# Longer contiguous runs for the expert weight loads of a hybrid encoder block with a mixture of experts

## Chip, cores and metric

One core of one Trainium2 chip runs the whole block, one layer, batch 1, 1,024 tokens of width 1,024, in float32. The metric is the device time of one execution in microseconds, as the median over runs.

## What is computed

The first half of the block mixes tokens (an input projection, a convolution branch, a gated linear attention branch, an output projection, a layer norm). The second half is a hierarchical mixture of experts: each token picks one group of 8 experts and in it 2 of 8 experts. Each of the 64 experts is a SwiGLU network with w1 and w3 of 1024 x 512 and w2 of 512 x 1024. The change touches this half alone.

```python
def hier_moe(x, w_rg, b_rg, w_re, b_re, w1, w3, w2):
    ...
    def expert_block(args):
        xb, e = args
        hdn = jax.nn.silu(xb @ w1[e]) * (xb @ w3[e])
        return hdn @ w2[e]
    ys = lax.map(expert_block, (xs, block_e)).reshape(n_slots, d) * slot_w[:, None]
    out = jnp.zeros((n_tok, d), x.dtype).at[slot_tok].add(ys)
```

## The kernel before

The engines run in program order; semaphores tie them together. The mixing half and the router take about the first 1,035 us. From then on the kernel goes through 29 tiles of 128 token rows in a fixed order (PATTERN). A tile holds one expert with 128 rows (letters r and o), two with 64 rows (s and d) or four with 32 rows (q). The 64 experts are ranked by their token counts on the chip, and the rank decides which of the three capacities an expert gets; 32 experts have 32 rows. One expert with more than 128 rows continues in the first d tile.

**Weights.** An expert's weights are six pieces of 1 MB: two of w1, two of w3, two of w2, in this order (w_pieces, line 924). load_piece (line 931) sends one piece into one of 22 slots of 128 partitions x 8 KB, some 16 of which serve the weights at a time. A half of w1 or w3 is 512 rows of 512 numbers: partition p gets rows p, 128 + p, 256 + p and 384 + p, each a run of 2 KB in memory. A half of w2 is 256 rows of 1,024 numbers: partition p gets rows p and 128 + p, each a run of 4 KB. pump_w (line 971) issues the next pieces on SyncE's queue as soon as TensorE has released as many slots: one after each quarter of a job's w1 and w3 products, two after its w2 products.

**A tile's tokens.** prep (line 1363) clears xgp and gathers the tile's 128 token rows into it from memory with an indirect DMA of GpSimd, one tile ahead. make_xt (line 1200) turns xgp into xT with eight 128 x 128 transposes on TensorE: transpose k takes columns k*128 to k*128 + 127, so that xT[:, k] has the inputs which the k-th 128 rows of w1 and w3 need. In a transpose the data is the loaded (stationary) operand.

**A job** is one expert on its rows. With T = 128 / rows (1, 2 or 4), job_h (line 1375) computes for each of 8 steps k and each of T column tiles j the product of xT[:, k] (stationary) with n = 512 / T columns of w1, then of w3; the column tile j writes its own 128 / T partitions of PSUM, so that the hidden columns j*n to (j+1)*n stand in the j-th partition group (line 1420). Each float32 product is two passes in the trace. ScalarE and VectorE then form silu(h1) * h3 in hs. job_t (line 1430) transposes hs in 4 / T pieces of 128 columns, and job_y (line 1438) multiplies with w2: step f takes the f-th 128 hidden numbers and the f-th 128 rows of w2. Transposes, w2 products and the scatter of finished tiles of the job before (combine, line 1487: products of one-hot matrices that add into the residual rows) are issued in between the 16 steps of the next job_h.

The last tile is a q tile. Its rows are finished apart (begin_last, add_last, last_rows), while the layer norm of all other rows goes out.

Of the kernel before, what the change touches and what calls it, by code (L numbers as in the profile page):

```python
# [28 lines left out]
DE = 512  # L29
# [25 lines left out]
assert (1 + N64) % 2 == 0 and N32 % 4 == 0  # L55
OVB = NT * 128
RND = float(3 << 22)


def _order():  # L60
# [22 lines left out]
def tile_block(ctx: ExitStack, tc: tile.TileContext, x, w_in, b_in, conv_w, conv_b, conv_ln_g,  # L83
# [5 lines left out]
    out = out[0]  # L89
# [13 lines left out]
    def slot(dt, name):  # L103
        return SP.tile([128, 2048], dt, tag="slot", name=name, bufs=NS)
# [13 lines left out]
    TE = nc.tensor  # L118
# [13 lines left out]
    ident = CP.tile([128, 128], F32, name="ident")  # L132
# [117 lines left out]
    def load_x(i):  # L250
        t = slot(F32, f"x{i}")
        for c in (slice(0, 512), slice(512, DM)) if i < 2 else (slice(0, DM),):
# [9 lines left out]
                      in_=w_in[:, C_F:C_F + 16].rearrange("(k p) c -> p k c", p=128))  # L262
# [606 lines left out]
    def mmb(shape=(128, 512), name="psb"):  # L869
        return PB.tile(list(shape), F32, tag="mm", name=name, bufs=5)  # L870
# [60 lines left out]
    def load_piece(wt, pc, t=None, eng=nc.sync):  # L931
        nm, src, i, e = pc
        if t is None:
            t = slot(F32, f"{nm}_{i}")
        if isinstance(e, int):
            m = src[e:e + 1]
        else:
            m = src[bass.ds(e(), 1)]
        r = 512 if nm != "w2" else 256
        f = 512 if nm != "w2" else 1024  # L940
        eng.dma_start(out=t.rearrange("p (k f) -> p k f", f=f),  # L941
                          in_=m.rearrange("o r f -> (o r) f")[i * r:(i + 1) * r].rearrange("(k p) f -> p k f", p=128))
        wt.setdefault(nm, []).append(t)

    rank_reg = {}
# [25 lines left out]
    def pump_w(eng=nc.sync):  # L971
        while queue and free[0] > 0 and (queue[0][0][0] == "s" or known):
            key, pc = queue.popleft()
            load_piece(wts_of[key], pc, eng=eng)
            free[0] -= 1
# [128 lines left out]
    xgp = CB.tile([128, DM], F32, name="xgp")  # L1104
# [95 lines left out]
    def make_xt(xT):  # L1200
        for h in range(2):
            ps = mmb((128, 4, 128), "psxT")
            for k in range(4):
                TE.transpose(ps[:, k, :], xgp[:, (4 * h + k) * 128:(4 * h + k + 1) * 128], ident)  # L1204
            A.copy(xT[:, 4 * h:4 * h + 4, :], ps)  # L1205

    static_map(0)
# [42 lines left out]
    V.tensor_scalar(c1[:, 0:16], i128[E64], ov, None, op0=OP.is_lt)  # L1250
    V.tensor_reduce(nb, c1[:, 0:16], axis=AX.X, op=OP.add)
    make_xt(rtm[:, 1024:2048].rearrange("p (k t) -> p k t", k=8))
    gather(tix[:, 1:2])
    prw = smb((128, 512), "psrow")
# [37 lines left out]
    rows = rt1[:, 832:1024].rearrange("p (a e) -> p a e", e=64)  # L1292
# [27 lines left out]
    V.tensor_scalar(hi, s16, -63.5, 1.0 / 128.0, op0=OP.add, op1=OP.mult)  # L1320
    V.tensor_scalar(hi, hi, RND, None, op0=OP.add)
    V.tensor_scalar(hi, hi, RND, None, op0=OP.subtract)
    V.scalar_tensor_tensor(lo, hi, -128.0, s16, op0=OP.mult, op1=OP.add)
# [47 lines left out]
    def turn_rows(s):  # L1371
        s["xT"] = WB.tile([128, 8, 128], F32, name="xTp", bufs=2)
        make_xt(s["xT"])

    def job_h(s, so, cap, wt, before=None, done=None, upto=16, nblk=0, after=None):


        T = 128 // cap
        n = DE // T
        if T == 1:  # L1380
            p1, p3 = mmb(name="psh1"), mmb(name="psh3")
        else:
            ps = mmb(name="psh")
            p1, p3 = ps[:, 0:n], ps[:, n:2 * n]
        whole = T == 1
        lag = 3 if fresh else 1
        fresh.clear()
        y_at = 8 if whole or nblk > 1 or after else 11
        for i, (p_, nm) in enumerate(((p1, "w1"), (p3, "w3"))):
            w_ = wt[nm]  # L1390
            for k in range(8):
                step = 8 * i + k
                if step == 4 and before and whole:
                    job_t(before)
                if step == 8:
                    if before and not whole:
                        if nblk:
                            cq.popleft()()
                        job_t(before)
                        for _ in range(nblk - 1):  # L1400
                            cq.popleft()()
                    elif whole:
                        for _ in range(nblk - 8):
                            cq.popleft()()
                    if after:
                        after()
                if step == y_at and before:
                    if whole and before["last"]:
                        while cq:
                            cq.popleft()()  # L1410
                    finish(before)
                    lag = step + 3 if fresh else lag
                    fresh.clear()
                if step >= lag:
                    if todo:
                        todo.popleft()()
                    elif whole and cq:
                        cq.popleft()()
                for j in range(T):
                    TE.matmul(p_[j * cap:(j + 1) * cap, :], s["xT"][:, k, so:so + cap],  # L1420
                                   w_[k // 4][:, (k % 4) * 512 + j * n:(k % 4) * 512 + (j + 1) * n],
                                   start=(k == 0), stop=(k == 7), skip_group_check=True)
                if done and k % 4 == 3 and step < upto:
                    done()
        hs = WB.tile([128, 512], F32, name="hs", bufs=2)
        A.activation(hs[:, 0:n], p1, AF.Silu)  # L1426
        V.tensor_tensor(hs[:, 0:n], hs[:, 0:n], p3, op=OP.mult)  # L1427
        return {"hs": hs, "T": T, "cap": cap, "wt": wt, "s": s, "so": so}

    def job_t(q):  # L1430
        nbk = 4 // q["T"]
        ps = mmb((128, 4, 128), "pshT")
        for c in range(nbk):
            TE.transpose(ps[:, c, :], q["hs"][:, c * 128:(c + 1) * 128], ident)  # L1434
        q["hT"] = WB.tile([128, 4, 128], F32, name="hT")
        A.copy(q["hT"][:, 0:nbk, :], ps[:, 0:nbk, :])  # L1436

    def job_y(q):
        if "hT" not in q:
            job_t(q)  # L1440
# [164 lines left out]
    def release(n):  # L1605
        free[0] += n
        pump_w()

    def finish(q):
        job_y(q)  # L1610
        if q["final"]:
            release(2)
        if q["last"]:
            combines(q["s"], q["oi"])

    class OnUse(dict):
# [5 lines left out]
        def __missing__(self, nm):  # L1622
            for pc in w_pieces(self.e):
                if pc[0] == nm:
                    load_piece(self, pc, self.tiles[pc[2]])
            return self[nm]

    def overflow():

        wtl = [slot(F32, f"wo{i}") for i in range(2)]  # L1630
        ovi = CB.tile([128, 1], F32, name="ovi")
        V.memset(ovi, float(NT))
        nblk = nc.values_load(ovt[0:1, 0:1], min_val=0, max_val=80)
        with tc.If(nblk > 0):  # L1634
            with tc.For_i(0, nblk, 1) as it:
                ev = nc.sync.value_load(ovt[0:1, bass.ds(it + 1, 1)], min_val=0, max_val=NE - 1)
                wt = OnUse(lambda: ev, wtl)
                oix = WB.tile([128, 1], I32, name="oix")
                ow = WB.tile([128, 1], F32, name="ow")
                otok = WB.tile([128, 1, 8], F32, name="otok")  # L1640
                pick(mark_of(ovi, 1, WB.tile([128, 112], BF16, name="obuf")), 1, oix, ow, otok)
                s = prep(oix, ow, otok[:, 0, :])
                turn_rows(s)
                job_y(job_h(s, 0, 128, wt))
                for f in combine([s]):
                    f()
                V.tensor_scalar(ovi, ovi, 1.0, None, op0=OP.add)
            G.memset(xgp, 0.0)
            gather(tix[:, 1:2])

    for oi, (ti, jobs) in enumerate(order):
# [43 lines left out]
        for ji_, (key, so, cap) in enumerate(jobs):  # L1695
            if oi == len(order) - 2 and ji_ == len(jobs) - 1:
                free[0] -= 2
            if oi == len(order) - 1:
# [3 lines left out]
                if ji_ == 1:  # L1702
                    while cq:
                        cq.popleft()()
                    while todo:
# [8 lines left out]
            nblk = -(-len(cq) // left)  # L1714
            after = next_rows if oi >= 2 and ji_ == len(jobs) - 1 and nx[0] is not None else None
            q = job_h(st[ti], so, cap, wts_of[key], pend, (lambda: release(1)) if final else None, 4 if held else 16,
                      nblk, after)
            q["final"], q["last"], q["oi"] = final, ji_ == len(jobs) - 1, oi
# [48 lines left out]
```

## Time and profile before

| what | value |
|---|---|
| median of 3 runs | 2072.95 us (2072.12 to 2077.11) |
| the profiled execution | 2076.78 us |
| its span, first to last instruction | 2075.0 us |
| TensorE busy in the span | 1952.7 us |
| moved by DMA in the span | 525.43 MB, of which the experts' weights are 384 pieces of 1.0486 MB = 402.7 MB |

The profile divides the span into 40 slices of 51.9 us. The first 20 are the mixing half and the router, the other 20 the experts. A busy TensorE is not a TensorE at its peak: the ends of its instructions are modelled, and each instruction's mean time contains its neighbours' overlap. The time of one of many equal instructions is therefore read from a piece of the chain of waits, as the length of the piece over its count.

### The profile page before, as it was taken

To read this page: it belongs to the slowest core of one execution; us is meant where nothing else is said; L and a number is where in the kernel's file an instruction comes from. 1 tells how busy PE (TensorE), PEld (TensorE's weight loads), DVE (VectorE), ACT (ScalarE), POOL (GpSimd) and SP (SyncE) were. 2 spreads that over 40 slices of the span, in tenths; PEclk is the share of its full clock that TensorE was granted. 3 is DMA by queue.
4 is the path that set the end of the run, shared out by engine and by line. 5 is a ranking of instruction groups with operands and counts; after the bars stand their busy time and mean duration, and the time that the engine had idled before them with its cause. 6 is when DMAs were issued, how large, how long until landed. Compare 5 with 4: busy or idle time off the path is not lost.

```text
span 2075.0 us, 34524 instructions
## 1 busy us (share of the span) xinstructions
PE 1952.7 (94%) x14631; PEld 1432.0 (69%) x14631; DVE 1023.6 (49%) x1483; ACT 507.6 (24%) x959; POOL 124.6 (6%) x130
## 2 busy tenths in 40 slices
PE   8999999999999999999898997999979997999686
PEld 6898889888888778899645565555655565555453
DVE  4777777878886475566631332223312332223156
ACT  5323342232222343211212121111121121121112
POOL 0000000000000130000100000000000000000000
PEclk9999999999999999999899998999999998999898
DMA  5101210243333536256799999999999999999995
GB/s 168 46 21 44 102 66 21 67 144 138 122 122 142 223 106 204 102 197 240 273 368 394 352 393 394 394 394 393 356 393 393 393 393 394 393 392 393 392 394 210
DMA packets 236749, 525.43 MB, mean 253 GB/s; under 512 B 11730, under 2 KB 53802, under 8 KB 236592
## 3 DMA queue, kind: packets, MB, share of 16 engines
q1 hardware_dynamic: 223808, 482.91, 63.0%
q0 software_dynamic: 12784, 40.28, 5.2%
q8 instruction: 116, 1.90, 0.4%
q14 instruction: 41, 0.34, 0.0%
HBM read 496.33 MB, written 34.08 MB: 256 GB/s over the span
## 4 chain that ended last, share of the span: by engine, by line
PE 37%; DMA 9%; DVE 2%; ACT 1%; issue 1%; SPq 1%; POOLq 0%; ACTq 0%
PE psh L1420 16%; PE pscb L1507 9%; DMA w<-in_w_dram 9%; PE psy L1455 6%; PE psy L1452 2%; PE psxT L1204 1%; PE psacc L1544 1%; PE pshT L1434 1%; DVE x L1512 1%; SPq L941 0%; ACT yv L1465 0%; ACT yhl L1484 0%; DVE yhl L1485 0%; PE psbc L1685 0%; DVE rtm L1337 0%
## 5 line engine op out<-in xcount | busy, mean ns | idle before, releaser
L1420 PE MATMUL psh<-w,xTp 128*32 128x128 f32 (+2 forms) x5792 | 442.0, 326 | 68.0 <-DMA w<-in_w_dram 61.6
L1420 PEld LDWEIGHTS psh<-w,xTp 128*32 128x32 f32 (+2 forms) x5792 | 269.9, 124 | 222.0 <-issue 107.6
L586 DVE SCALAR_TENSOR_TENSOR c<-sg,cw,c 128x994 f32<-128x994 f32 (+14 forms) x240 | 310.0, 1292 | 5.4
L1512 DVE TENSOR_TENSOR x<-x,pscb 128x512 f32<-128x512 f32 x240 | 164.2, 687 | 231.1 <-PE pscb L1507 230.5
L1507 PE MATMUL pscb<-yhl,pt 128*128 128x512 f32 x896 | 268.5, 443 | 8.6 <-DVE pt L1500 6.8
L1507 PEld LDWEIGHTS pscb<-yhl,pt 128*128 128x128 f32 x896 | 162.4, 197 | 93.8 <-issue 33.0
L1455 PE MATMUL psy<-w,hT 128*32 128x256 f32 (+1 forms) x1408 | 150.6, 445 | 0.8 <-ACT hT L1436 0.8
L1427 DVE TENSOR_TENSOR hs<-hs,psh 128x128 f32<-128x128 f32 (+2 forms) x65 | 25.4, 391 | 235.6 <-ACT hs L1426 210.3
L1465 ACT COPY yv<-psy 32x256 f32<-32x256 f32 (+1 forms) x174 | 73.7, 423 | 213.2 <-PE psy L1455 211.3
L1436 ACT COPY hT<-pshT 128x128 f32<-128x128 f32 (+2 forms) x65 | 22.8, 350 | 365.6 <-PE pshT L1434 365.6
L1455 PEld LDWEIGHTS psy<-w,hT 128*32 128x32 f32 (+1 forms) x1408 | 56.6, 118 | 71.8 <-issue 51.7
L1485 DVE SCALAR_TENSOR_TENSOR yhl<-yv,tw,yhl 128x1024 fp32r<-128x1024 f32 x19 | 24.4, 1284 | 160.0 <-ACT yhl L1484 150.9
L1364 POOL MEMSET xgp<- 128x1024 f32 x27 | 25.7, 953 | 828.4 <-PE psxT L1204 828.4
L1452 PE MATMUL psy<-w,hT 128*128 128x512 f32 x144 | 64.0, 597 | 0.0
L1485 DVE SCALAR_TENSOR_TENSOR yhl<-psy,tw,yhl 128x512 fp32r<-128x512 f32 x18 | 13.5, 750 | 88.6 <-ACT yhl L1484 87.6
L1205 ACT COPY xTp<-psxT 128x512 f32<-128x512 f32 x56 | 30.1, 590 | 109.4 <-PE psxT L1204 108.9
L1452 PEld LDWEIGHTS psy<-w,hT 128*128 128x128 f32 x144 | 26.8, 190 | 32.5 <-issue 31.2
L1500 DVE TENSOR_TENSOR pt<-iof,ttok 128x256 fp32r<-128x256 f32 (+1 forms) x120 | 47.8, 400 | 0.0
L1426 ACT ACTIVATE hs<-psh 128x128 f32<-128x128 f32 (+2 forms) x65 | 23.5, 361 | 56.8 <-PE psh L1420 56.3
L1204 PEld LDWEIGHTS psxT<-ident,xgp 128*128 128x128 f32 x232 | 27.4, 143 | 9.1 <-issue 4.1
L1204 PE MATMUL psxT<-ident,xgp 128*128 128x128 f32 x232 | 31.1, 278 | 2.4 <-DVEq L1634 1.6
L502 DVE SCALAR_TENSOR_TENSOR st<-st,dec,pskv 128x256 f32<-128x256 f32 x60 | 28.8, 480 | 7.2 <-PE pskv L218 4.0
(653 smaller groups left out, 3849.1 us busy)
## 6 DMA issues: line engine op xcount, KB each, us to landing
w<-in_w_dram SPq DMA_DIRECT2D x382, 1024.0 KB, 14.0
x<-in_x_dram SPq DMA_DIRECT2D x6, 1024.0 KB, 8.2
o_d<-oT POOLq DMA_DIRECT2D x4, 1024.0 KB, 4.4
conv_d<-c POOLq DMA_DIRECT2D x4, 1024.0 KB, 4.7
or<-o_d SPq DMA_DIRECT2D x4, 1024.0 KB, 4.7
og_d<-or POOLq DMA_DIRECT2D x4, 1024.0 KB, 5.2
gb_d<-gb POOLq DMA_DIRECT2D x4, 1024.0 KB, 7.4
o<-og_d SPq DMA_DIRECT2D x4, 1024.0 KB, 5.8
```

The lines of the kernel that those rows point to most:

```text
L502: V.scalar_tensor_tensor(o, prev, gla["dec", p][:, hh, c:c + 1], pk[b][:, a, :], op0=OP.mult, op1=OP.add)
L586: V.scalar_tensor_tensor(c[:, s:], u[:, :SEQ - s], w, c[:, s:], op0=OP.mult, op1=OP.add)
L1204: TE.transpose(ps[:, k, :], xgp[:, (4 * h + k) * 128:(4 * h + k + 1) * 128], ident)
L1205: A.copy(xT[:, 4 * h:4 * h + 4, :], ps)
L1420: TE.matmul(p_[j * cap:(j + 1) * cap, :], s["xT"][:, k, so:so + cap], w_[k // 4][:, (k % 4) * 512 + j * n:(k % 4) * 512 + (j + 1) * n], st ...
L1452: TE.matmul(pys[h], lh, w_[:, h * 512:(h + 1) * 512], start=(f == 0), stop=(f == 3))
L1455: TE.matmul(pys[0][j * cap:(j + 1) * cap, 0:n], lh, w_[:, j * n:(j + 1) * n], start=(f == 0), stop=(f == 3), skip_group_check=True)
L1465: (V.tensor_copy if j % 2 and "same" in s and q["last"] else A.copy)(s["y"][so:so + cap, j * n:(j + 1) * n], pys[0][j * cap:(j + 1) * cap, ...
L1485: V.scalar_tensor_tensor(s["hl"][:, 1024 + c:1024 + c + n], y, s["w"], f32(hi), op0=OP.mult, op1=OP.subtract)
L1500: V.tensor_tensor(pts[tt][:, 0:n, :], iof[:, None, :].to_broadcast([128, n, 128]), tk[:, :, None].to_broadcast([128, n, 128]), op=OP.is_equal)
L1507: TE.matmul(ps, pts[tt][:, a, :], s["hl"][:, i * 1024 + h * 512:i * 1024 + (h + 1) * 512], start=(a + i == 0), stop=(a == n - 1 and i == 1))
L1512: V.tensor_tensor(xa, xa, ps, op=OP.add)
```

## The change

All three weights are read with `(p k) f -> p (k f)`: partition p takes neighbouring rows (4 of w1 or w3, 2 of w2), which are one run of 8 KB in memory and one run of 8 KB in the slot. The number of DMAs, their bytes, their order and their slots stay.

The k-th 128 rows that a step sees are now rows 4p + k of a half instead of 128k + p, so the other operand is put in the same order. make_xt's transposes take every fourth column of xgp's halves (a step of 16 bytes in a partition). The hidden numbers have to come in w2's new order (rows 2p + k of a half): for T = 1 and T = 2 the transposes of hs in job_t take every second column (a step of 8 bytes); for T = 4 each of the four column tiles of w1 and w3 reads every second column of a 256-column half (a step of 8 bytes in the moving operand), and the transpose of hs stays as it was. No instruction is added or removed on TensorE, ScalarE or VectorE.

```diff
--- before.py
+++ after.py
@@ -55,6 +55,7 @@
 assert (1 + N64) % 2 == 0 and N32 % 4 == 0
 OVB = NT * 128
 RND = float(3 << 22)
+RUNS = ("w1", "w3", "w2")
 
 
 def _order():
@@ -938,8 +939,12 @@
             m = src[bass.ds(e(), 1)]
         r = 512 if nm != "w2" else 256
         f = 512 if nm != "w2" else 1024
-        eng.dma_start(out=t.rearrange("p (k f) -> p k f", f=f),
-                          in_=m.rearrange("o r f -> (o r) f")[i * r:(i + 1) * r].rearrange("(k p) f -> p k f", p=128))
+        rows = m.rearrange("o r f -> (o r) f")[i * r:(i + 1) * r]
+        if nm in RUNS:
+
+            eng.dma_start(out=t, in_=rows.rearrange("(p k) f -> p (k f)", p=128))
+        else:
+            eng.dma_start(out=t.rearrange("p (k f) -> p k f", f=f), in_=rows.rearrange("(k p) f -> p k f", p=128))
         wt.setdefault(nm, []).append(t)
 
     rank_reg = {}
@@ -1201,7 +1206,7 @@
         for h in range(2):
             ps = mmb((128, 4, 128), "psxT")
             for k in range(4):
-                TE.transpose(ps[:, k, :], xgp[:, (4 * h + k) * 128:(4 * h + k + 1) * 128], ident)
+                TE.transpose(ps[:, k, :], xgp[:, h * 512 + k:(h + 1) * 512:4], ident)
             A.copy(xT[:, 4 * h:4 * h + 4, :], ps)
 
     static_map(0)
@@ -1418,7 +1423,7 @@
                         cq.popleft()()
                 for j in range(T):
                     TE.matmul(p_[j * cap:(j + 1) * cap, :], s["xT"][:, k, so:so + cap],
-                                   w_[k // 4][:, (k % 4) * 512 + j * n:(k % 4) * 512 + (j + 1) * n],
+                                   w_[k // 4][:, (k % 4) * 512:(k % 4 + 1) * 512][:, part(T, j)],
                                    start=(k == 0), stop=(k == 7), skip_group_check=True)
                 if done and k % 4 == 3 and step < upto:
                     done()
@@ -1427,11 +1432,18 @@
         V.tensor_tensor(hs[:, 0:n], hs[:, 0:n], p3, op=OP.mult)
         return {"hs": hs, "T": T, "cap": cap, "wt": wt, "s": s, "so": so}
 
+    def every2(c):
+        return slice(c // 2 * 256 + c % 2, c // 2 * 256 + 256, 2)
+
+    def part(T, j):
+
+        return every2(j) if T == 4 else slice(j * (DE // T), (j + 1) * (DE // T))
+
     def job_t(q):
         nbk = 4 // q["T"]
         ps = mmb((128, 4, 128), "pshT")
         for c in range(nbk):
-            TE.transpose(ps[:, c, :], q["hs"][:, c * 128:(c + 1) * 128], ident)
+            TE.transpose(ps[:, c, :], q["hs"][:, 0:128] if q["T"] == 4 else q["hs"][:, every2(c)], ident)
         q["hT"] = WB.tile([128, 4, 128], F32, name="hT")
         A.copy(q["hT"][:, 0:nbk, :], ps[:, 0:nbk, :])
```

## Rows read from the trace of the kernel before

**Rows 1.** The page: TensorE; GB/s in 40 slices; all packets; an instruction-loading DMA queue.

```profile
PE 1952.7 (94%) x14631; PEld 1432.0 (69%) x14631; DVE 1023.6 (49%) x1483; ACT 507.6 (24%) x959; POOL 124.6 (6%) x130
GB/s 168 46 21 44 102 66 21 67 144 138 122 122 142 223 106 204 102 197 240 273 368 394 352 393 394 394 394 393 356 393 393 393 393 394 393 392 393 392 394 210
DMA packets 236749, 525.43 MB, mean 253 GB/s; under 512 B 11730, under 2 KB 53802, under 8 KB 236592
q8 instruction: 116, 1.90, 0.4%
```

**Rows 2.** SyncE's weight loads, line 941: ns min/median/max each; then issue to landing.

```profile
L941 SPq DMA_DIRECT2D w<-in_w_dram x382: 367/2198/6328, 921.7 to 2030.6; - x191
DMA to landing us min/median/max: 5.8/14.0/17.8
```

**Rows 3.** TensorE's waits (us, times, longest): whole; 1035-1305; 1500-1983; 1542-1772.

```profile
PE psh L1420 <- DMA w<-in_w_dram: 61.6, 28, 5.4
...
PE psh L1420 <- DMA w<-in_w_dram: 19.5, 8, 4.8
...
PE psh L1420 <- DMA w<-in_w_dram: 42.0, 20, 5.4
...
PE psh L1420 <- DMA w<-in_w_dram: 13.1, 6, 4.3
```

**Rows 4.** Stretches of 25 us: engines' busy time, granted clock, DMA share, GB/s.

```profile
1150.00:1175.00 25.00, 25.00 (x131) 15.16 (x131) 10.16 (x18) 3.22 (x7) 0.27 (x1) 1.00 0.85 304
...
1450.00:1475.00 25.00, 25.00 (x145) 14.64 (x141) 7.57 (x15) 2.72 (x5) 0.00 (x0) 1.00 0.98 361
1475.00:1500.00 25.00, 25.00 (x259) 15.75 (x262) 8.29 (x15) 5.15 (x9) 1.95 (x2) 1.00 0.94 347
```

**Rows 5.** Timeline of TensorE: products that waited for weights, idle time before in brackets.

```profile
1118.11 6.54 PE L1420 MATMUL psh<-w,xTp 128*128 128x512 f32 x8 [4.67 <-DMA w<-in_w_dram]
...
1304.86 2.05 PE L1420 MATMUL psh<-w,xTp 128*128 128x512 f32 x2 [2.26 <-DMA w<-in_w_dram]
...
1540.80 5.09 PE L1420 MATMUL psh<-w,xTp 128*64 128x256 f32 x32 [5.19 <-DMA w<-in_w_dram]
...
1770.80 1.10 PE L1420 MATMUL psh<-w,xTp 128*128 128x512 f32 x2 [2.38 <-DMA w<-in_w_dram]
...
1981.94 0.43 PE L1420 MATMUL psh<-w,xTp 128*32 128x128 f32 x8 [1.22 <-DMA w<-in_w_dram]
```

**Rows 6.** Stretches of 2 us, columns as before: w1/w3, w2, w1/w3.

```profile
1606.00:1608.00 2.00, 2.00 (x15) 1.31 (x12) 0.13 (x1) 0.00 (x0) 0.00 (x0) 1.00 1.05 385
1614.00:1616.00 2.00, 2.00 (x14) 1.52 (x15) 1.30 (x2) 0.61 (x2) 0.14 (x1) 1.00 1.04 413
1620.00:1622.00 2.00, 2.00 (x22) 1.29 (x18) 0.00 (x0) 0.58 (x2) 0.00 (x0) 1.00 1.06 387
```

**Rows 7.** The whole experts' half as one stretch, same columns.

```profile
1043.00:2050.00 1007.00, 924.95 (x8526) 559.71 (x8529) 293.17 (x510) 185.48 (x394) 53.80 (x56) 0.96 1.03 387
```

**Rows 8.** Chain of waits (start, us): 32-row job's products; tile's transposes; router's products.

```profile
1668.35 3.49 PE psh L1420 x128
...
1317.39 0.87 PE psxT L1204 x8
...
1044.14 1.39 PE psval L1346 x48
```

**Rows 9.** Groups by line and shape: busy us, mean ns; idle before, releasers.

```profile
L1420 PE MATMUL psh<-w,xTp 128*32 128x128 f32 x4096 | 138.9, 284 | 47.0 <-DMA w<-in_w_dram 40.8 <-issue 5.9 <-ACT xTp L1205 0.2
L1204 PEld LDWEIGHTS psxT<-ident,xgp 128*128 128x128 f32 x232 | 27.4, 143 | 9.1 <-issue 4.1 <-ACTq L1634 2.0 <-DMA xgp<-x_d,tix 0.9
L1434 PEld LDWEIGHTS pshT<-ident,hs 128*128 128x128 f32 x116 | 14.8, 144 | 17.9 <-issue 8.3 <-DVE hs L1427 4.9 <-PE pscb L1507 1.7
```

**Rows 10.** The token gathers: landing time (us) among DMA issues; TensorE's waits for them.

```profile
xgp<-x_d,tix POOLq DMA_INDIRECT x29, 7.1
...
PE psxT L1204 <- DMA xgp<-x_d,tix: 0.8, 1, 0.8
```

## Prediction

> **What bounds the kernel now.** I read the page first. TensorE is busy for 94% of the span, which looks like the bound [rows 1]. The same page's GB/s line says otherwise for the experts' half: from the 21st slice on it stands at 392 to 394 in nearly every slice, dips to 352 and 356 in two, and falls only in the last [rows 1]. A rate so flat over 1,000 us, whatever the tiles hold, is a limit of the transfers. SyncE agrees: a weight load that takes 0.37 us to issue when there is room takes 2.2 us in the median, and lands 14 us after issue [rows 2], which is the time of five pieces; there is always a queue. The waits give the other side: TensorE stood idle for weights 28 times, 61.6 us in all, 19.5 of them before 1305 us and 42.0 after 1500 [rows 3].
>
> The time is set by DMA from the moment the loads were last held back for want of a slot to TensorE's last wait for weights before they are held back again. The loads were held back where the rate dips, near 1175 and between 1450 and 1500 [rows 4]; TensorE's waits end at 1118, 1305 and 1982 [rows 5]. So there are three DMA-set stretches: A, about 1040 to 1118 (78 us), B, 1175 to 1305 (130 us), C, 1500 to 1982 (482 us). In between, and from 1982 to the end, TensorE sets the time.
>
> **What longer runs are worth.** In the trace a packet is one run: the page counts 236,749 packets, nearly all under 8 KB [rows 1], and 256 pieces x 512 plus 128 x 256 of them are the weights' 163,840. Where only w1 and w3 move, the rate is 385 to 387; where w2 moves it touches 413 [rows 6]. The small windows blur at their edges, so I take w2's rate from the mean: with two thirds of the bytes at 386 and a mean of 393, the last third moves at 1 / (3/393 - 2/386) = 408 GB/s. On one of 16 engines a 2 KB packet then takes 2048 x 16 / 386 = 84.9 ns and a 4 KB packet 160.6 ns: 75.7 ns for each 2 KB and 9.2 ns for the packet. Drawn out to 8 KB: 9.2 + 4 x 75.7 = 312 ns, or 420 GB/s. A piece of 1.0486 MB takes 2.717 us at 386, 2.570 at 408 and 2.497 at 420. An expert costs 4 x 2.717 + 2 x 2.570 = 16.01 us now and 6 x 2.497 = 14.98 us then: 1.03 us less.
>
> No row has an 8 KB packet of weights, so this has bounds. The engines do carry longer packets: the instruction queue's 116 packets hold 1.90 MB, 16 KB each [rows 1]. If the loads are cut at 4 KB all the same, all pieces run at 408 and an expert saves 4 x 0.147 = 0.59 us. Below nothing: if 8 KB runs move no faster than w1 does, w2 loses 2 x 0.147 = 0.29 us an expert. At w2's peak of 413 instead of 408 the same line gives 427 GB/s and 1.14 us from the mean-based cost. I take 1.03, since it goes through both measured sizes.
>
> With the gathers between them experts follow each other every 16.1 us. A holds 5, B 8, C 30. Wanted: A 5.1, B 8.2, C 30.9 us.
>
> **What TensorE can give.** A DMA-set stretch shrinks only as far as TensorE's idle time in it. In A it is 4.7 us [rows 5], so A gives 4.7. A and B together hold 19.5 us [rows 3]; B gives its 8.2. C has 42.0 for 30.9 [rows 3], unevenly: up to the wait that ends at 1541 it wants 2.6 us, up to 1771 14.7, up to 1982 13.5. Waits fall in the q tiles, whose four experts are all load and little work, and between 1541 and 1771 they hold 13.1 us [rows 3]; I take 2 us off. That makes 4.7 + 8.2 + 29 = 42 us. The clock may return a little: its mean is 0.96 in the half [rows 7], the full level (2.4 GHz) with falls to half (1.2 GHz) around the waits; fewer waits leave it up for longer. I count nothing for it.
>
> **What the strides cost.** All strided reads are TensorE's, and no row of before has a float32 operand with a step. (1) The products of 32-row jobs: 4,096 passes, 3.49 us a job [rows 8], 32 jobs. Bounds: nothing, or twice as long (112 us in all). The nearest row is the router's product that takes its columns in pairs with a step between pairs: 48 passes in 1.39 us [rows 8], 29 ns each, where 128 passes of the job take 27 ns each. Those are narrow bfloat16 columns, so it only says that a step by itself doesn't stall. In DMA-set stretches a q tile's experts wait for their weights anyway, and that idle time is the cover; the four jobs of the last tile have none. (2) The tile's transposes with a 16 byte step: eight loads of 143 ns [rows 9] beside eight passes that take 0.87 us together [rows 8], 29 tiles. (3) The transposes of hs with an 8 byte step, 84 of the 116 (one in each 32-row job stays), 144 ns a load [rows 9]. For (2) and (3) the bounds are nothing and one more load time of about 0.11 us each: 25 us and 9 us. A gain is excluded for all three, since they read the same bytes in the same instructions. I take nothing for them but 2 us for the uncovered places.
>
> The Trainium skill speaks to these steps. "SBUF — State Buffer", Door 1: The DMA port swizzle, says that SBUF is read in lines of 16 bytes and that full rate needs two or more accesses to a line. By it the 8 byte step is free and the 16 byte step of the tile's transposes is not; no run here shows it, and the result is the second rival below.
>
> **Other edges.** A gather is 128 rows of 4 KB, eight on each of 16 engines. If each stood behind one weight packet, of 312 instead of 85 ns, it would land 1.8 us later than its 7.1 us [rows 10]. Gathers are issued a tile ahead and TensorE waited 0.8 us for them in all [rows 10]: no cost. If that cover went, 29 x 1.8 = 52 us would be exposed. SyncE issues the same loads in the same order; the static experts' first pieces arrive in the router's time and wait for it.
>
> **Sum.** 42 - 2 = 40 us off the profiled execution's 2076.78, 2036.8; off the median, which is 3.8 us below it, 2033.
>
> **Rivals.**
> First, the runs are cut at 4 KB: 43 experts x 0.59 = 25 us, 2048. For it: no packet on this queue is longer now. Against it: the 16 KB packets of another queue. The Trainium skill's "DMA: Bandwidth & Descriptors", SWDGE vs HWDGE vs iDMA, gives a packet as 4096 bytes preferably, for descriptors that software writes; these loads are SyncE's, so the trace neither agrees nor disagrees yet.
>
> Second, the tile's transposes load at half pace: 0.87 us a tile. Eight tiles turn in the stretches that TensorE sets: 7 us. The other 21 cost 18 us, of which the idle time that is left (61.6 - 42, about 20 us, all in q tiles) covers half: 9. Gain 40 - 16 = 24, 2049. This is what the Trainium skill's line rule ("SBUF — State Buffer", Door 1) would make of the transposes.
>
> Third, slower than before: all strided operands are read at half pace and TensorE becomes the bound throughout. Added work 112 + 25 + 9 = 146 us. TensorE has 1007 - 925 = 82 us of idle time in the half [rows 7], and 20 us more if the clock never fell (4% of 1007 at half speed): 44 to 64 us slower, about 2125. It turns slower from some 82 to 102 us of added work on, that is if the strided reads took 1.6 to 1.7 times as long.
>
> Fourth, 8 KB runs move at 386, no better than 2 KB: 43 x 0.29 = 13 us slower, 2086. Nothing in the trace points there; what speaks for it is only that memory is walked in an order of which no row shows the rate.
>
> **Numbers.** Forecast 0.58, first rival 0.14, second 0.15, third 0.05, fourth 0.04, and 0.04 for a gain of up to 15 us from mixed costs. Predicted is the forecast's 2033. Its own range is 2020 (w2's peak rate with the clock's return, some 53 us) to 2044; up to 2054 takes in the first two rivals and leaves out the other 0.13 and some tails. A change of 0.3%, 6.2 us, is about what a measurement here can tell. Faster: 0.58 + 0.14 + 0.15 + 0.02 = 0.89; within: 0.03; slower: 0.05 + 0.03 = 0.08.
>
> **What would show it.** If each run is one packet the page counts 236,749 - 163,840 + 49,152 = 122,061 packets, cut at 4 KB 171,213. The GB/s line should stand near 420, or near 408. The waits for weights should fall from 61.6 us to about 20 and the dips in the rate should grow, since the loads catch up with TensorE sooner. A 32-row job's chain piece should stay at 3.49 us and line 1204's load at 143 ns. The prediction is wrong if the rate rises and the span doesn't: then TensorE, not DMA, was the bound in C, and the products or the transposes will be longer.

## The result and the profile after

The changed kernel takes 2038.24 us in the median (four runs, 2037.92 to 2038.77), the kernel before 2073.27 us beside it (2072.12 to 2077.11): a ratio of 0.9828, 95% interval 0.9811 to 0.9845, which is 35 us. The profiled execution took 2038.77 us with a span of 2037.0 us, so the two profiled spans differ by 38.0 us. The forecast was 2033 with an own range of 2020 to 2044: the direction and the mechanism hold, the size was 5 us too large.

The page of the changed kernel, with the rows that answer to [rows 1]: TensorE, its granted clock in tenths, GB/s in 40 slices of 50.9 us, all packets.

```profile
PE 1946.1 (96%) x14630; PEld 1435.9 (70%) x14631; DVE 1024.0 (50%) x1483; ACT 507.8 (25%) x959; POOL 124.2 (6%) x130
PEclk9999999999999999999899999999999999999898
GB/s 171 42 27 45 104 53 37 51 119 177 118 99 111 241 145 172 126 215 207 232 349 407 378 419 420 420 420 398 318 410 420 377 405 419 420 420 420 419 418 171
DMA packets 122573, 525.43 MB, mean 258 GB/s; under 512 B 11730, under 2 KB 53802, under 8 KB 73264
```

The flat level of 392 to 394 has become 419 to 420, the rate that was drawn out from the two shorter sizes. The packets fell by 114,176: each 8 KB run is one packet. And the line is less flat: slices at 398, 318, 410, 377 and 405 stand where before only single ones dipped. There the loads were held back for want of a slot: between 1400 and 1480 us and between 1600 and 1650 SyncE waited before its weight loads for TensorE alone (69.5 and 44.7 us, waits that began earlier included), where between 1700 and 1740 it waited 28.9 of 29.7 us for transfers.

TensorE's waits for weights in the changed kernel (us in total, times, longest), which answer to [rows 3]: whole; 1035 to 1500; 1500 to 1983.

```profile
PE psh L1425 <- DMA w<-in_w_dram: 29.7, 15, 5.4
...
PE psh L1425 <- DMA w<-in_w_dram: 8.3, 5, 4.1
...
PE psh L1425 <- DMA w<-in_w_dram: 21.4, 10, 5.4
```

The prediction wanted about 20 us here; 29.7 are left.

The timeline of TensorE in the changed kernel (start, length, instruction; idle time before it and what ended it in brackets), with the five places that answer to [rows 5], and behind the first of them the start of a job that is used further down:

```profile
1113.58 3.67 PE L1425 MATMUL psh<-w,xTp 128*128 128x512 f32 x8 [0.39 <-ACT hs L1431]
...
1159.05 7.13 PE L1425 MATMUL psh<-w,xTp 128*64 128x256 f32 x64
...
1289.40 1.10 PE L1425 MATMUL psh<-w,xTp 128*128 128x512 f32 x2 [1.02 <-DMA w<-in_w_dram]
...
1522.96 5.22 PE L1425 MATMUL psh<-w,xTp 128*64 128x256 f32 x32 [5.42 <-DMA w<-in_w_dram]
...
1743.00 1.10 PE L1425 MATMUL psh<-w,xTp 128*128 128x512 f32 x2 [2.93 <-DMA w<-in_w_dram]
...
1929.69 1.94 PE L1425 MATMUL psh<-w,xTp 128*32 128x128 f32 x32 [1.36 <-DMA w<-in_w_dram]
```

Cutting both traces at these places gives stages that hold the same work. In the next two views the columns are: stretch, its length, busy time and instruction count of PE, PEld, DVE, ACT and POOL, granted TensorE clock, DMA share, GB/s. First the kernel before (the last cut at 1969, behind the waits of the last but one tile), with three stretches of 25 us at the end:

```profile
1043.00:1118.00 75.00, 64.49 (x938) 39.88 (x937) 20.69 (x43) 16.89 (x38) 5.92 (x6) 0.97 1.03 390
1118.00:1305.00 187.00, 167.90 (x1773) 106.29 (x1774) 49.08 (x87) 33.77 (x77) 9.75 (x10) 0.95 1.02 382
1305.00:1541.00 236.00, 223.38 (x1655) 131.52 (x1657) 60.46 (x103) 42.43 (x85) 13.65 (x14) 0.98 1.02 385
1541.00:1771.00 230.00, 216.87 (x1972) 134.18 (x1971) 64.19 (x113) 40.20 (x87) 13.65 (x14) 0.96 1.04 393
1771.00:1969.00 198.00, 179.58 (x1447) 107.61 (x1450) 49.32 (x85) 35.01 (x69) 9.75 (x10) 0.97 1.04 393
1969.00:2075.00 106.00, 83.33 (x946) 46.57 (x938) 58.45 (x91) 21.47 (x48) 2.13 (x3) 0.89 0.80 304
...
1043.00:2075.00 1032.00, 935.54 (x8719) 566.05 (x8718) 302.19 (x522) 189.78 (x404) 54.84 (x57) 0.96 1.01 380
...
1100.00:1125.00 25.00, 18.55 (x299) 11.77 (x292) 0.57 (x2) 5.22 (x15) 1.95 (x2) 0.86 1.05 392
...
1600.00:1625.00 25.00, 25.00 (x152) 15.20 (x151) 9.77 (x19) 4.75 (x9) 1.95 (x2) 1.00 1.04 392
1625.00:1650.00 25.00, 25.00 (x124) 13.57 (x126) 7.99 (x12) 4.35 (x7) 1.96 (x2) 1.00 1.04 395
```

Then the changed kernel, with five stretches of 25 us at the end (those near 1150, 1425 and 1600 answer to [rows 4]):

```profile
1043.00:1113.50 70.50, 65.28 (x937) 40.89 (x933) 19.55 (x42) 16.16 (x37) 5.33 (x6) 0.98 1.00 405
1113.50:1289.40 175.90, 164.12 (x1772) 105.68 (x1773) 49.32 (x88) 33.76 (x78) 9.76 (x10) 0.98 0.99 408
1289.40:1523.00 233.60, 221.81 (x1655) 132.46 (x1655) 60.50 (x103) 42.43 (x85) 13.65 (x14) 1.00 0.97 391
1523.00:1743.00 220.00, 213.65 (x1972) 133.93 (x1972) 64.12 (x113) 40.21 (x87) 13.66 (x14) 0.99 0.99 407
1743.00:1930.00 187.00, 179.30 (x1447) 109.05 (x1451) 49.26 (x85) 35.02 (x69) 9.75 (x10) 0.98 1.02 420
1930.00:2037.00 107.00, 84.55 (x946) 46.67 (x938) 58.53 (x91) 21.55 (x48) 2.12 (x3) 0.88 0.73 300
...
1043.00:2037.00 994.00, 928.70 (x8718) 568.68 (x8714) 301.28 (x522) 189.13 (x403) 54.28 (x57) 0.98 0.96 394
...
1100.00:1125.00 25.00, 23.13 (x339) 14.67 (x331) 0.58 (x2) 7.70 (x21) 3.90 (x4) 1.00 1.01 418
...
1150.00:1175.00 25.00, 25.00 (x164) 13.99 (x166) 4.07 (x7) 4.71 (x9) 1.95 (x2) 1.00 0.85 336
...
1425.00:1450.00 25.00, 25.00 (x123) 12.60 (x123) 4.78 (x8) 4.21 (x7) 0.00 (x0) 1.00 0.81 286
...
1600.00:1625.00 25.00, 25.00 (x117) 14.24 (x114) 6.93 (x12) 3.21 (x7) 2.69 (x3) 1.00 0.86 339
1625.00:1650.00 25.00, 25.00 (x257) 14.59 (x259) 7.03 (x12) 5.20 (x9) 0.00 (x0) 1.00 0.97 384
```

The counts of PE agree stage by stage (938 and 937, 1773 and 1772, 1655, 1972, 1447, 946), so the lengths can be subtracted: the six stages gave 4.5, 11.1, 2.4, 10.0, 11.0 and -1.0 us, 38.0 in all. Two things are to be read here besides the lengths. In the fifth stage nothing holds the loads back in either kernel, and 198 us at 393 GB/s became 187 at 420 (198 x 393 / 420 = 185). In the fourth the rate after is only 407, because of the dip at 1600, which the kernel before did not have. The dips at 1150 and 1425, at 336 and 286 GB/s, lie where before had its own.

Over the whole half, TensorE's idle time fell from 1032 - 935.5 = 96.5 us to 994 - 928.7 = 65.3, by 31.2. Its busy time, for the same instructions, fell by 6.8. That second part goes with the clock, whose mean went from 0.96 to 0.98.

### The profile page after: what moved, and what is told of

It reads as the page before. It is cut to its first block, busy times and chain, and to the rows that moved or that the text cites. A ratio compares the mean times of both kernels' runs of the same rounds, so it can differ in the third digit from the quotient of the medians.

```text
span 2037.0 us, 34524 instructions
## 1 busy us (share of the span) xinstructions
PE 1946.1 (96%) x14630; PEld 1435.9 (70%) x14631; DVE 1024.0 (50%) x1483; ACT 507.8 (25%) x959; POOL 124.2 (6%) x130
## 2 busy tenths in 40 slices
DMA packets 122573, 525.43 MB, mean 258 GB/s; under 512 B 11730, under 2 KB 53802, under 8 KB 73264
## 3 DMA queue, kind: packets, MB, share of 16 engines
q0 software_dynamic: 12528, 40.28, 5.3%
## 5 line engine op out<-in xcount | busy, mean ns | idle before, releaser
L1425 PE MATMUL psh<-w,xTp 128*32 128x128 f32 (+2 forms) x5792 | 437.8, 324 | 35.8 <-DMA w<-in_w_dram 29.7
L1519 PE MATMUL pscb<-yhl,pt 128*128 128x512 f32 x896 | 262.5, 435 | 9.1 <-DVE pt L1512 7.5
L1519 PEld LDWEIGHTS pscb<-yhl,pt 128*128 128x128 f32 x896 | 157.5, 192 | 92.9 <-DVE x L1524 32.7
L1497 DVE SCALAR_TENSOR_TENSOR yhl<-yv,tw,yhl 128x1024 fp32r<-128x1024 f32 x19 | 24.4, 1284 | 150.6 <-ACT yhl L1496 150.6
L1209 PEld LDWEIGHTS psxT<-ident,xgp 128*128 128x128 f32 x232 | 32.3, 208 | 8.1 <-issue 3.7
```

What stands on the lines that cost most here:

```text
L1209: TE.transpose(ps[:, k, :], xgp[:, h * 512 + k:(h + 1) * 512:4], ident)
L1497: V.scalar_tensor_tensor(s["hl"][:, 1024 + c:1024 + c + n], y, s["w"], f32(hi), op0=OP.mult, op1=OP.subtract)
L1519: TE.matmul(ps, pts[tt][:, a, :], s["hl"][:, i * 1024 + h * 512:i * 1024 + (h + 1) * 512], start=(a + i == 0), stop=(a == n - 1 and i == 1))
```

## The experiments

The theory was that of the prediction: transfers set three stretches, longer runs move faster, and the strides cost next to nothing because TensorE waits there anyway. Against it stood that the strides eat a part of the gain, that only a part of the lengthening counts, and that something other than the loads sets the time.

**The changed kernel again**, without an edit, as the measure for the three that follow.

> The changed kernel once more, beside the three runs that take it apart, so that they are compared on one chip. Expected: 2038 us, ratio 0.983 to the kernel before.

Measured: 2037.52 us, ratio 0.9824 (0.9807 to 0.9841); waits for weights 29.6 us. The first result repeats.

**Long runs with plain reads.**

```diff
-                TE.transpose(ps[:, k, :], xgp[:, h * 512 + k:(h + 1) * 512:4], ident)
+                TE.transpose(ps[:, k, :], xgp[:, (4 * h + k) * 128:(4 * h + k + 1) * 128], ident)
...
-        return every2(j) if T == 4 else slice(j * (DE // T), (j + 1) * (DE // T))
+        return slice(j * (DE // T), (j + 1) * (DE // T))
...
-            TE.transpose(ps[:, c, :], q["hs"][:, 0:128] if q["T"] == 4 else q["hs"][:, every2(c)], ident)
+            TE.transpose(ps[:, c, :], q["hs"][:, c * 128:(c + 1) * 128], ident)
```

> All loads in runs of 8 KB, but TensorE reads without steps, as the kernel before did; rows and columns of the weights then don't meet the right inputs, so the values differ. Theory (the strides cost little, the gain is the loads'): the trace of the changed kernel prices the strides at 0.24 us for each of 32 jobs of 32 rows, 0.08 us for each of 29 tiles and 0.02 us for each of 84 transposes of hs, 12 us of TensorE's work, of which only the part in TensorE's own stretches shows: 2033 to 2037 us. Rival (the shortfall of 5 us against the forecast, and more, is strides): below 2030 us. Second rival (all of it is hidden by the loads): 2038 us.

Measured: 2035.28 us, 0.9802 (0.9783 to 0.9821), 2.2 us below the changed kernel beside it by the medians and 4.6 by the ratios (0.0022 of 2074 us); the intervals overlap. Waits 31.2 us. So the strides cost some 2 to 5 us in place, which is not clear of nothing, and the rivals that let them eat half of the gain or more are out.

**Strided reads with the old loads.**

```diff
-RUNS = ("w1", "w3", "w2")
+RUNS = ()
```

> The loads of the kernel before (runs of 2 and 4 KB) with the changed kernel's strided reads; values differ for the same reason as in e1_plain_reads. Theory: 12 us of added work in a kernel that waits 62 us for weights shows as 1 to 4 us: 2074 to 2077 us. Rival (strides cost what the rows don't show, by other reads of the same memory): above 2085 us. The transfers' rate should stay at 392 to 394 GB/s in the experts' half.

Measured: 2076.37 us, 1.0009 (0.9999 to 1.0019). In the profiled execution the waits for weights were 52.0 us instead of 61.6, the flat level of the rate stayed at 392 to 394. Here TensorE had more work and the time hardly rose, as it should if the work is spent out of waiting time: seen from the other side, the cover that the prediction named. The size of the fall in the waits shows less, since this execution was the fastest of twelve (2070.03 us) and that of the kernel before a long one (2076.78).

**w1 and w3 alone in long runs.** Then w2 keeps 4 KB runs and only the tile's transposes have a step.

```diff
-RUNS = ("w1", "w3", "w2")
+RUNS = ("w1", "w3")
...
-        return every2(j) if T == 4 else slice(j * (DE // T), (j + 1) * (DE // T))
+        return slice(j * (DE // T), (j + 1) * (DE // T))
...
-            TE.transpose(ps[:, c, :], q["hs"][:, 0:128] if q["T"] == 4 else q["hs"][:, every2(c)], ident)
+            TE.transpose(ps[:, c, :], q["hs"][:, c * 128:(c + 1) * 128], ident)
```

> Only w1 and w3 in runs of 8 KB, w2 in 4 KB as before; of the strides only that of the tile's transposes is needed. Theory (time goes by 9.2 ns a packet): an expert costs 4 x 2.497 + 2 x 2.570 = 15.13 us, 0.88 of the 1.03 us, so 0.85 of the gain of 35 us, and some 2 us less for strides: 2041 to 2044 us, rate about 416 GB/s. Rival (the gain comes only when all runs are alike, since short packets hold up long ones): 2050 us or more.

Measured: 2038.76 us, 0.9832 (0.9815 to 0.9849), against 0.9824 for all three. The page of this kernel, GB/s and packets:

```profile
GB/s 173 46 22 45 104 64 25 60 109 185 118 91 118 240 139 172 130 212 208 232 351 410 378 415 417 416 415 404 319 408 415 394 403 415 415 416 416 415 416 198
DMA packets 138958, 525.43 MB, mean 258 GB/s; under 512 B 11731, under 2 KB 53803, under 8 KB 106033
```

The rate is what the sizes give: four pieces at 420 and two at 408 make 6 / (4/420 + 2/408) = 416. The time came out 2 us or more below what was expected of it. Within the intervals w2's longer runs, and the strided products and transposes of hs that they ask for, cancel: this smaller change does as well.

**Runs of 4 KB for all.**

```diff
-            eng.dma_start(out=t, in_=rows.rearrange("(p k) f -> p (k f)", p=128))
+            eng.dma_start(out=t.rearrange("p (a f) -> p a f", a=2), in_=rows.rearrange("(a p b) f -> p a (b f)", a=2, p=128))
...
-                TE.transpose(ps[:, k, :], xgp[:, h * 512 + k:(h + 1) * 512:4], ident)
+                TE.transpose(ps[:, k, :], xgp[:, h * 512 + k // 2 * 256 + k % 2:h * 512 + k // 2 * 256 + 256:2], ident)
```

With it, `RUNS` and the reads of w1, w3 and hs are those of the experiment above.

> w1 and w3 in runs of 4 KB (two per partition and half), w2 in 4 KB as before. Theory (9.2 ns a packet and 75.7 ns for each 2 KB): all pieces at 408 GB/s, 0.59 us an expert saved, 25 us forecast for this case before the result, scaled by the 35 measured for 40 forecast 22: 2048 to 2052 us. Rival (2 KB is the only size that is slow): 2040 us or less. Rival (packets have to be 8 KB): 2070 us.

Measured: 2048.03 us, 0.9878 (0.9858 to 0.9897), beside a kernel before of 2071.36 us, as are the three that follow. Waits 38.2 us. The page, and the two kinds of transposes among the groups (busy us, mean ns; idle before and what ended it), where the tile's transposes now step by 8 bytes and those of hs not at all:

```profile
GB/s 170 47 22 44 104 67 21 65 107 182 123 83 134 247 112 171 150 189 217 231 371 408 386 407 409 408 408 397 322 407 409 393 396 408 408 408 408 408 408 210
DMA packets 171725, 525.43 MB, mean 257 GB/s; under 512 B 11730, under 2 KB 53802, under 8 KB 171568
...
L1209 PEld LDWEIGHTS psxT<-ident,xgp 128*128 128x128 f32 x232 | 32.2, 207 | 8.1 <-issue 3.7 <-ACTq L1646 2.0 <-DMA xgp<-x_d,tix 1.0
L1446 PEld LDWEIGHTS pshT<-ident,hs 128*128 128x128 f32 x116 | 14.7, 143 | 17.8 <-issue 8.2 <-DVE hs L1432 4.9 <-PE pscb L1519 1.7
```

408 GB/s for 4 KB runs, as taken from the mixed trace of before. The three sizes, 386, 408 and 420, lie on one line of a fixed price per packet and one per byte, and the time follows the rate: this is what the first rival would have looked like. The order in which memory is walked changes along with the length of the runs, and no run here parts the two.

**Half of the loads, plain and strided.** Every second expert works with its neighbour's weights and loads none, so that TensorE never waits for weights; the first with plain reads, the second with the strides of the change.

```diff
+                if len(seen) % 2 == 0:
+                    same_as[key] = last_key[0]
+                    wts_of[key] = wts_of[last_key[0]]
+                    continue
...
-            uses[key] -= 1
+            uses[same_as[key]] -= 1
```

The plain one also has the three plain reads shown further up.

> Every second expert uses the weights of the expert before it and loads none, so half of the weights' bytes are not moved; 8 KB runs, reads without steps. It shows the time that TensorE alone would need. Theory (DMA sets the stretches A, B and C): the 62 us of waits for weights and about 20 us of half clock go: about 1990 us. Rival (TensorE is the bound and its waits are an accident of the profile): above 2025 us.

> As e5_half_loads_plain (every second expert uses its neighbour's weights), with the changed kernel's strided reads. With no wait to hide them the strides show in full. Theory: 12 us above e5_half_loads_plain, about 2002 us. Rival (strides cost more than their rows): over 25 us above it.

Measured: 1987.32 us plain, 0.9589 (0.9571 to 0.9607), and 1994.92 us strided, 0.9628 (0.9611 to 0.9645). The strides cost 7.6 us where nothing covers them, less than the 12 that were expected: those rested on 0.24 us a job, which is what the changed kernel's pieces of 3.67 us for 126 passes come to at 128. From the chain of waits of the plain one (start, length, what), then its experts' half as one stretch:

```profile
1549.24 0.58 PE pshT L1453 x4
...
1636.02 3.49 PE psh L1432 x128
...
1643.68 0.87 PE psxT L1216 x8
...
1043.00:1985.80 942.80, 906.10 (x8725) 550.99 (x8722) 302.77 (x523) 189.84 (x404) 54.79 (x57) 0.99 0.57 209
```

and the same of the strided one:

```profile
1549.33 0.68 PE pshT L1453 x4
...
1644.46 0.95 PE psxT L1216 x8
...
1689.54 3.63 PE psh L1432 x128
...
1043.00:1991.30 948.30, 914.65 (x8701) 562.03 (x8697) 301.02 (x521) 188.81 (x402) 53.79 (x56) 0.99 0.56 207
```

A 32-row job's products take 0.14 us longer (4%), a tile's eight transposes 0.08, four strided transposes of hs 0.10. Over 32 jobs, 29 tiles and 84 transposes that is 4.5 + 2.3 + 2.1 = 8.9 us. The two stretches above don't hold the same work (8725 and 8701 instructions); counted from the first transposes of a tile on, 1042.62 and 1040.38 us, where both hold 8726, TensorE is busy for 906.5 us in the plain one and 917.0 in the strided one, 10.5 more. The strides are priced: some 9 or 10 us of work, of which some 2 to 5 were exposed in the changed kernel.

These two also give the limit: 1995 us is what TensorE alone needs with the strides, 43 us below the changed kernel, which waits for weights only 29.7 us.

**Another order of the tiles.** If the time lost in the dips is the loads' loss, an order that never holds them back should win it. This one puts tiles with much loading and tiles with much work closer together.

```diff
-PATTERN = "ssqrdqoqoddoodqdodoqoqoddddqq"
+PATTERN = "ssqrqddoqddodqodoqoqooqoddddq"
```

> The changed kernel with another order of the same 29 tiles: ssqrqddoqddodqodoqoqooqoddddq. Theory (the loads are held back near 1160, between 1400 and 1475 and near 1610 us because several tiles that are heavy for TensorE follow each other, about 28 us of transfer time at 420 GB/s): with the heavy tiles spread between the q tiles the loads run through and most of that comes back: 2006 to 2016 us. Rival (held-back loads are made up for later, since q tiles wait anyway): 2035 us or more.

Measured: 2038.81 us, 0.9840 (0.9822 to 0.9858): nothing gained on the changed kernel. The page's GB/s, TensorE's waits for weights, the last of them in the timeline, and the half cut there:

```profile
GB/s 171 45 24 45 104 53 36 48 121 173 119 102 104 240 153 172 118 224 203 236 331 415 399 419 420 420 420 420 415 419 420 419 420 419 402 420 419 420 280 148
...
PE psh L1425 <- DMA w<-in_w_dram: 21.1, 10, 4.2
...
1676.49 1.94 PE L1425 MATMUL psh<-w,xTp 128*32 128x128 f32 x32 [1.36 <-DMA w<-in_w_dram]
...
1170.00:1185.00 15.00, 9.54 (x192) 7.18 (x188) 0.29 (x1) 3.87 (x11) 1.95 (x2) 0.77 1.01 420
...
1676.00:2033.00 357.00, 328.76 (x2722) 195.46 (x2722) 129.65 (x213) 66.69 (x137) 17.71 (x19) 0.97 0.88 358
...
1043.00:2032.80 989.80, 927.73 (x8710) 570.14 (x8706) 301.75 (x521) 188.81 (x402) 53.80 (x56) 0.98 0.96 395
```

The order did what it was made for: the dips are gone, and the loads end earlier (280 instead of 418 in the 39th slice). But the waits fell by 8.6 us only, all of them before 1676, and then TensorE alone set the time for 357 us while the loads ran ahead to no use. Against the half loads this kernel is 41.5 us longer in the half (989.8 - 948.3): 28.4 us more idle, 21.1 of it these waits, and 13.1 us more busy time for the same instructions. So the expectation fell, and the time is the rival's (2035 us or more): loads that never stop are not enough, the waits have to go, and here all that are left come early. Whether another order has fewer was not tried.

## Why the prediction was right, and where it was off

**Where the time is set.** Right. The rate was the limit, the three DMA-set stretches shrank, and the two half loads show the other limit, TensorE's, 84 us (plain) and 76 us (strided) below the kernel before. That "the rate rises and the span doesn't" did not come.

**What longer runs are worth.** Right in the terms that the sum uses: 420 GB/s drawn out, 419 to 420 measured; 408 for 4 KB, 407 to 409 measured with 4 KB runs alone. Of the packets 122,061 were forecast and 122,573 counted. The 512 between them are the two pieces that GpSimd issues: its queue's packets fell by 256, from 12,784 to 12,528, so these two moved before in 512 packets, not in the 1,024 that were subtracted for them. A packet of that queue held 4 KB, two runs. The first rival (cut at 4 KB) and the fourth (no faster than 2 KB) are out. What the Trainium skill says of a packet ("DMA: Bandwidth & Descriptors", SWDGE vs HWDGE vs iDMA: 4096 bytes preferably) fits GpSimd's two pieces before and bound neither queue after: SyncE's and GpSimd's both sent 8 KB. Two slips in the working don't touch the sum: at w2's peak rate the saving is 16.01 - 6 x 1.0486 / 427 = 1.27 us an expert, not 1.14, and the 21st slice stands at 368, below the level.

**The stretches.** Here is the term that was mis-sized, C: 29 us of loading were forecast and 24.4 came. A was to give 4.7 us and gave 4.5.

B was to give 8.2 and its stage gave 11.1, but the loads gave what was forecast. The stage begins at 1118, B at 1175, and what lies between was TensorE's: behind the wait at 1118 the first eight products took 6.54 us before, in a stretch with a granted clock of 0.86, and 3.67 after, in one at 1.00. That is 2.9 us. The rest can be cut at the start of a job in the dip, which is this one in the kernel before and stands at 1159.05 in the view of the changed one:

```profile
1166.30 7.13 PE L1420 MATMUL psh<-w,xTp 128*64 128x256 f32 x64
```

From there to the end of the wait that ends the stage, 1304.86 - 1166.30 = 138.6 us became 1289.40 - 1159.05 = 130.4, which is the 8.2.

C was to give 29 us, and what comes behind it none. Its three stages gave 2.4 + 10.0 + 11.0 and the tail took 1.0: 22.4. Call the lead how much earlier the changed kernel starts the same instruction. The 2.4 up to 1541 look like the 2.6 that were wanted, but that is luck. The lead grew by 1.6 us behind the wait at 1305, where the products were slow again (the first two took 2.05 us, and 1.10 after); it fell by 1.2 from one tile's transposes to another's (1317.23 to 1514.95 before, 1300.17 to 1499.13 after), in the part that TensorE sets, where the strides are exposed and plain reads let it stay (17.3 and 17.6 us); and the loads gave 2.0 up to 1541.

The stage up to 1771 wanted 14.7 us and gave 10.0. The prediction held C for DMA-set from end to end, and it was not any more: with the loads faster, they caught up with TensorE at 1600 and were held back there (339 GB/s in that stretch, 384 in the next, where before 392 and 395 stood). From the transposes at 1536.25 to those at 1684.36 (1553.95 and 1700.71 before) TensorE set the time, and the strides took 1.4 us of the lead; from there on the loads gave 11.4. Missing from 420 the two stretches cost 25 x (81 + 36) / 420 = 7 us of loading, of which 14.7 - 11.4 = 3.3 show; where the rest was made up stays open. The prediction said that the dips would grow, but gave no price for it: its 2 us taken off stood for idle time that runs out, not for loads held back. The last stage gave 11.0 of the 12.7 that were wanted up to 1969; from 1930 on TensorE set the time and nothing was to be won. Taken together the loads gave 4.5 + 8.2 + 2.0 + 11.4 + 11.0 = 37.1 us of the 42, and what is missing is C's.

**What the strides cost.** The sum's 2 us are within what was measured in place (2.2 us by the medians, 4.6 by the ratios, with overlapping intervals). The step behind it failed: "A 32-row job's chain piece should stay at 3.49 us and line 1204's load at 143 ns." Both grew: the piece to 3.63 us in the strided half loads (3.67 for 126 passes in the changed kernel), the load to 208 ns. The transposes' loads in the changed kernel, to be set beside [rows 9] (all 232 of the tiles with a step of 16 bytes; 84 of the 116 of hs with a step of 8):

```profile
L1209 PEld LDWEIGHTS psxT<-ident,xgp 128*128 128x128 f32 x232 | 32.3, 208 | 8.1 <-issue 3.7 <-ACTq L1646 2.0 <-DMA xgp<-x_d,tix 1.0
L1446 PEld LDWEIGHTS pshT<-ident,hs 128*128 128x128 f32 x116 | 18.6, 188 | 16.5 <-issue 8.1 <-DVE hs L1432 4.6 <-PE pscb L1519 1.7
```

From 143 to 208 ns with 16 bytes; and (188 x 116 - 144 x 32) / 84 = 205 ns with 8. With runs of 4 KB the tile's transposes stepped by 8 bytes and took 207. So the loads came out inside the bounds, near the middle. Little of that shows in the time, 0.08 us for the eight transposes of a tile, or 10 ns of the 65 each, since loads and products overlap in the trace; the work is 9 or 10 us in all. Most of it stayed hidden because TensorE waits for weights: an edit that is costed at nothing for its cover costs 7.6 us when the loads are halved.

The second rival took the line rule of the Trainium skill ("SBUF — State Buffer", Door 1) for the 16 byte step alone, since two numbers of 4 bytes lie in a line at a step of 8. The runs agree with it in that a step of 16 bytes slows a read, but not in the rest: a step of 8 slows the load as much (207 against 208 ns), the products at a step of 8 lose 4%, and neither comes near half pace, a size that was the prediction's own. Its price of 16 us fell with that, and so did the third rival's 146 us, against 9 or 10 measured.

**The clock.** "I count nothing for it" was the third size that was off. TensorE's idle time fell by 31.2 us, not by the 42 of the sum; its busy time fell although the strides added to it. Counted from the first transposes of a tile on, 8726 instructions in each trace, the kernel before has 936.5 - 906.5 = 30.0 us more busy time than the plain half loads, and 61.6 us of waits; the changed kernel has 930.3 - 917.0 = 13.3 more than the strided half loads, and 29.7 us of waits. So some 17 us of work came back (14 by the repeat of the changed kernel, 933.3 us). A microsecond of waiting went with about half a microsecond more work: 0.45 to 0.63 over the runs with waits that share their reads with one of the half loads.

The half loads also move half the bytes, so slower work beside more traffic would look alike; the granted clock speaks for the clock. Its mean over the span is 0.973 before, 0.983 after and 0.989 in both half loads. A TensorE at work throughout would lose 2.7% of 2075 us, 1.7% of 2037 and 1.1% of the two others at these means, an estimate of 56, 35 and 22 us, so 34 and 13 more than the half loads, beside the 30.0 and 13.3. The third rival's 20 us for a clock that never falls were too few: 4% of 1007 us is 40 at most, and 30 are measured. The rows behind that are stretches at less than the full level: in the other order the 15 us from 1170 on, with 5.5 us idle, ran at a mean of 0.77.

Inside a DMA-set stretch the clock only decides how much of the transfers' time shows as idle and how much as slower work. Behind the last wait of such a stretch it sets the time itself: the 2.9 us at 1118 and the 1.6 at 1305.

**The number.** The working gave 2036.8 for a profiled execution, which took 2038.77: 2 us off. Part of that is luck. The loads gave some 5 us less than the sum had and the exposed strides with the tail took 3.6 us instead of 2, while 4.5 us of faster work, not in the sum, made up for most of it. The remaining 3 us to the median came from taking over the distance between profiled run and median, 3.8 us before, 0.5 us after.

## What to carry to other kernels

Where the rate of a load stream is flat over stages of different work, count its packets: two run lengths in one trace give a price per packet and one per byte, and the line through them foretold a run of twice the length to the GB/s. Do not carry the saving straight to the end of the kernel: a faster stream runs into its slots earlier, so reckon for each stretch where it will be held back next, and price that, and with it the slower work that follows the last wait of a stretch. And an operand's step is cheap only as long as its engine waits for something else; price it in a variant in which that wait is gone.

## What was not expected of the hardware

The weight load of a 128 x 128 float32 transpose took 143 ns plain, 207 ns with a step of 8 bytes and 208 with one of 16: the step itself costs, not its size, for these two. Float32 products whose moving operand steps by 8 bytes took 3.63 us for 128 passes instead of 3.49.

Waits went with more than their length: 61.6 us of waits came with 30 us of slower work, and 29.7 us with 13.
